# Softmax on negated scores in a windowed attention: the sink as the start of the minimum and as one more column

## The chip, the core and the metric

The kernel runs on one core of a Trainium2 chip. The time is device microseconds from start to end of the program. Five engines of the core work side by side, each through its own queue and in its order: PE (matrix products), DVE (VectorE), ACT (ScalarE), POOL (GpSimd) and SP, which here only issues DMAs. The profile tells for every instruction its start, its duration and, from the semaphores, what ended a wait before it.

## The reference, cut to what matters

One layer of a bidirectional encoder is computed for two requests, a prompt of 512 tokens and a sample of 1024, with shared weights: RMSNorm, one projection, windowed attention beside a convolution branch, an output projection, a feed-forward part with a short convolution, a last RMSNorm. The attention, which is what the change touches, is:

```python
sc = einsum("bnqhgd,bnkhd->bnhgqk", qb, kb) * (HEAD_DIM ** -0.5)
sc = sc + bias[None, None]
sc = where(mask, sc, NEG)                       # |q - k| <= 128 and inside the sequence
sk = sink.reshape(N_KV, GROUP, 1, 1)
m = maximum(max(sc, axis=-1, keepdims=True), sk)
p = exp(sc - m)
denom = sum(p, axis=-1, keepdims=True) + exp(sk - m)
p = (p / denom)
o = einsum("bnhgqk,bnkhd->bnqhgd", p, vb)
```

Queries come in blocks of 128. Each block sees its own 128 keys and the 128 on both sides (256 keys at the ends of a sequence, 384 elsewhere). There are 8 heads in 2 groups of 4, each group with its own keys and values. The sink is one number per head; it takes part in the maximum and in the denominator, and has no value row.

## The kernel before

All matrix products are made of operands split into a high and a low part: ACT writes the rounded high part (L143, L548), and POOL or DVE subtracts it from the original to get the low part (L144, L549). PE then multiplies high by high, high by low and low by high, which is why most PE lines come in threes (L250, L251 and L253 for the projections and the up-projection; L813 to L815 for the down-projection). For a chunk of weights, `split` has ACT cast 128x1024 elements (L143) and POOL subtract (L144); PE needs POOL's result for L253.

The work is written as Python generators which are advanced in turn. The main line is the projection (`step`) and later the prompt's feed-forward part (`ffn_step`); attention, the normalisation of the convolution branch and the output projection are put between its matrix products by `tick`, at rates given by constants. So the prompt's attention, 4 blocks, stands beside the sample's projection (about 115 to 255 us of the profile), and the sample's, 8 blocks, beside the prompt's feed-forward part (about 390 to 760 us). The depthwise convolution over 31 taps, which DVE does tap by tap (L293), runs in between as well, with some taps on ACT and POOL (L285, L286). After that come the output projection of the sample (L641 to L643) and the sample's feed-forward part, in a form with fewer products.

The order of instructions in each engine's queue up to there is not written out by hand. A planner takes the program and orders each engine's instructions by its own estimate of durations, in the limits of the dependences. For the last part (from L1202 on) the order on PE is by hand and the planner orders the other engines.

A unit of attention is one block of queries for one group of 4 heads; there are 12 blocks and 2 groups, 24 units. For a unit, `scores` does this for each of the 4 heads: two matmuls give the scores in a PSUM bank (L502); one DVE instruction adds the bias, writes the sum to a tile `p` in SBUF, and keeps the row's maximum (L505, followed in the trace by a short read of the accumulator). After all four heads:

- L512 (DVE) takes the minimum of the negated maximum and the negated sink, for four columns at once: `negm`, the negative of the softmax's maximum.
- L513 (DVE) adds the sink to it: the exponent of the sink's term.
- L515 (ACT, four times) takes the exponential of each head's row with `negm` as bias and sums it into `den`.
- L517 (ACT) takes the exponential of the sink's term, L518 (DVE) adds it to `den`, L519 (DVE) takes the reciprocal.
- L523 and L525 multiply each head's row by it: three heads on ACT and one on POOL in the prompt, and one on DVE, two on ACT, one on POOL in the sample.

`values` then transposes the rows on PE (L546), splits them (L548, L549), multiplies by the values (L560, L561) and combines the result (L568 to L572). A unit's scores are made before the values of the unit ahead of it, so that PE has other work while the softmax runs.

Other lines that the prediction speaks of: L775 is a tap of the short convolution in the feed-forward part, on DVE, which reads a PSUM bank; PE's next product into that bank (L250) waits for it. L127 is a small scaling on POOL, L319 a small memset on POOL, L323 the gate of the convolution branch on DVE. `qsd` is a buffer in DRAM through which the queries go.

The tiles in SBUF come from fixed slots, taken when a tile is made and given back when its last holder goes; a new tile's first writer waits until the former tile's readers are done.

## Time and profile before

| | |
|---|---|
| median of 3 runs | 1566.0 us (1565.88 to 1571.18) |
| profiled execution | 1563.92 us |
| its span, first to last instruction | 1562.1 us |
| mean granted PE clock | 0.998 |
| instructions | 20200 |
| attention of the prompt, 8 units | about 115 to 255 us |
| attention of the sample, 16 units | about 390 to 760 us |

A line of the page or of a view names the source line, the engine, the operation and the tiles (out<-in, buffer numbers left out), then shapes and the number of instructions. In a view of one line the three durations are minimum, median and maximum in nanoseconds. In a view of waits "PE a L561 <- DVE h L549: 1.7, 3, 1.2" says that PE's line 561, writing a tile of kind a, waited for DVE's line 549 for 1.7 us in total, in 3 waits, the longest 1.2 us. In a timeline the first number is the start in us from the span's start, the second the duration. Matmuls overlap in their pipeline: one of 128x512 shows a duration of about 0.39 us but the next starts some 0.23 us after it.

### The profile page before, as it was taken

What the parts mean: (1) busy time and instruction counts of PE and PEld (TensorE: products, weight loads), DVE (VectorE), ACT (ScalarE), POOL (GpSimd) and SP (SyncE); (2) the same over time, 40 slices, a digit from 0 to 9 for tenths busy, and PEclk for the clock granted to TensorE, in tenths of its full rate; (3) what the DMA queues carried; (4) which work ended last, traced back from release to release, by engine and by line L of the source; (5) the groups of instructions that cost most, each with busy time, mean ns of one, the idle gap of its engine ahead of it and who ended that gap; (6) DMA issues with size and microseconds to landing.
All of it is one profiled execution on the core that took longest, in us unless ns stands there. A gap on an engine that the chain in (4) does not pass through costs nothing. (4 is left out here: it accounts for less than half of the span.)

```text
span 1562.1 us, 20200 instructions
## 1 busy us (share of the span) xinstructions
PE 1519.2 (97%) x6909; PEld 1234.5 (79%) x6909; DVE 1200.5 (77%) x1731; ACT 799.2 (51%) x1426; POOL 729.5 (47%) x559
## 2 busy tenths in 40 slices
PE   8899899999998999999999999999999999999998
PEld 6787788887886778888877887888888878788886
DVE  7999868638989996756675768777777777877795
ACT  4634566335565655656554455444444445544364
POOL 7651344238576676656653324555555554000135
PEclk9999999999999999999999999999999999999999
DMA  7573246446331333333657222333333332694642
GB/s 229 157 201 95 87 118 165 130 133 166 108 117 64 108 108 109 99 97 95 212 164 230 82 68 78 111 102 101 101 102 102 101 102 101 206 354 144 219 142 108
DMA packets 209771, 207.62 MB, mean 133 GB/s; under 512 B 11156, under 2 KB 150748, under 8 KB 209541
## 3 DMA queue, kind: packets, MB, share of 16 engines
q1 hardware_dynamic: 209669, 206.35, 42.0%
q8 instruction: 54, 0.88, 0.2%
q14 instruction: 48, 0.39, 0.1%
HBM read 158.84 MB, written 48.51 MB: 133 GB/s over the span
## 5 line engine op out<-in xcount | busy, mean ns | idle before, releaser
L144 POOL TENSOR_TENSOR q<-q,q 128x1024 fp32r<-128x1024 f32 x72 | 175.0, 2436 | 68.8 <-ACT q L143 33.8
L921 POOL TENSOR_TENSOR q<-q,q 128x512 fp32r<-128x512 f32 x82 | 114.0, 1401 | 155.9 <-ACT q L1031 151.4
L250 PE MATMUL u<-h,q 128*128 128x512 f32 x400 | 158.5, 396 | 3.6 <-DVE h L775 2.8
L251 PE MATMUL u<-h,q 128*128 128x512 f32 x400 | 158.6, 396 | 0.6 <-DVE h L212 0.6
L253 PE MATMUL u<-h,q 128*128 128x512 f32 x384 | 151.9, 396 | 2.2 <-POOL q L144 2.2
L1045 PE MATMUL w<-h,q 128*128 128x512 f32 x372 | 147.4, 396 | 3.1 <-ACT h L1126 1.7
L1047 PE MATMUL w<-h,q 128*128 128x512 f32 x372 | 145.9, 392 | 0.6 <-POOL q L921 0.6
L293 DVE SCALAR_TENSOR_TENSOR c<-c,cvw,c 128x512 f32<-128x512 f32 x184 | 138.1, 750 | 2.4
L1046 PE MATMUL w<-h,q 128*128 128x512 f32 x350 | 137.6, 393 | 0.0
L143 ACT CAST q<-q 128x1024 fp32r<-128x1024 f32 x72 | 75.6, 1050 | 77.5 <-POOL q L144 44.6
L918 POOL TENSOR_TENSOR q<-q,q 128x1024 f32<-128x1024 f32 x8 | 23.8, 2989 | 182.9 <-DVE q L918 171.2
L250 PE MATMUL b<-h,q 128*128 128x512 f32 x256 | 102.1, 399 | 2.9 <-DVE d L323 2.9
L1354 PE MATMUL w<-h,h 128*128 128x512 f32 x264 | 103.8, 393 | 0.0
L1356 PE MATMUL w<-h,h 128*128 128x512 f32 x264 | 103.6, 392 | 0.0
L921 DVE TENSOR_TENSOR h<-h,h 128x512 fp32r<-128x512 f32 (+1 forms) x128 | 92.3, 764 | 11.4 <-ACT h L925 9.2
L251 PE MATMUL b<-h,q 128*128 128x512 f32 x256 | 100.7, 393 | 0.0
L253 PE MATMUL b<-h,q 128*128 128x512 f32 x256 | 100.5, 393 | 0.0
L1355 PE MATMUL w<-h,h 128*128 128x512 f32 x244 | 95.9, 393 | 0.0
L921 POOL TENSOR_TENSOR c<-q,c 128x512 fp32r<-128x512 f32 x46 | 71.0, 1557 | 51.8 <-ACT c L1031 51.8
L250 PEld LDWEIGHTS u<-h,q 128*128 128x128 f32 x400 | 75.6, 189 | 20.4 <-DVE h L775 3.3
L925 ACT CAST h<-h 128x512 fp32r<-128x512 f32 x101 | 58.7, 618 | 59.4 <-DVE h L921 27.0
L251 PEld LDWEIGHTS u<-h,q 128*128 128x128 f32 x400 | 75.5, 189 | 16.4 <-DVE h L212 1.6
(457 smaller groups left out, 4278.8 us busy)
## 6 DMA issues: line engine op xcount, KB each, us to landing
q<-in_w_up SPq DMA_DIRECT2D x88, 512.0 KB
h<-in_w_down SPq DMA_DIRECT2D x90, 256.0 KB
ga<-q SPq DMA_DIRECT2D x64, 256.0 KB
h<-ga SPq DMA_DIRECT2D x57, 256.0 KB
q<-in_w_in SPq DMA_DIRECT2D x28, 512.0 KB
q<-in_x_sample SPq DMA_DIRECT2D x15, 512.0 KB
h<-qsd SPq DMA_DIRECT2D x24, 256.0 KB
q<-ga SPq DMA_DIRECT2D x20, 256.0 KB
```

Of the source, the lines that this page charges most:

```text
L144: (nc.vector if dve else nc.gpsimd).tensor_tensor(lo[:], raw[:], hi[:].bitcast(F32), op=ALU.subtract)
L250: nc.tensor.matmul(out, whi[:, kc, :], hi[:], start=(kc == 0), stop=False)
L251: nc.tensor.matmul(out, whi[:, kc, :], lo[:], start=False, stop=False)
L253: nc.tensor.matmul(out, wlo[:, kc, :], hi[:], start=False, stop=(kc == KC - 1))
L293: nc.vector.scalar_tensor_tensor(acc[:], src(t), w(t), acc[:], op0=ALU.mult, op1=ALU.add)
L921: (eng or nc.vector).tensor_tensor(out, a, b, op=ALU.subtract)
L1045: nc.tensor.matmul(out, whi[:, s], hi[:], start=(start and c == 0), stop=False, **go)
L1046: nc.tensor.matmul(out, whi[:, s], lo[:], start=False, stop=False, **go)
L1047: nc.tensor.matmul(out, wlo[:, s], hi[:], start=False, stop=(stop and c == 3), **go)
L1354: nc.tensor.matmul(out, sh[:, c], th[:], start=(p == 0), stop=False)
L1355: nc.tensor.matmul(out, sh[:, c], tl[:], start=False, stop=False)
L1356: nc.tensor.matmul(out, sl[:, c], th[:], start=False, stop=(p == NPAIR - 1))
```

## The change

The scores' sum with the bias is written negated, and the row's minimum is kept instead of its maximum. That minimum starts from the negated sink of the head, given as a pointer to one number per partition, so it is `negm` at once. The row's tile is one column longer, and POOL copies the negated sink into that column. The exponential is taken with a scale of -1 over the longer row, so its sum, the denominator, has the sink's term in it. L512, L513, L517 and L518 have nothing left to do and are gone, and so are the two small tiles `mx` and `es`. The transposes and products after it use the row without its last column, as before.

```diff
-        mx, negm, den, es = sm(GRP), sm(GRP), sm(GRP), sm(GRP)
-        hs = slice(kv * GRP, (kv + 1) * GRP)
+        negm, den = sm(GRP), sm(GRP)
         pr = []
         for j in range(GRP):
             h = kv * GRP + j
...
-            p = sb.tile([3 * P])
+            p = sb.tile([3 * P + 1])
+            nc.gpsimd.tensor_copy(p[:, nk:nk + 1], nsink[:, h:h + 1])
             nc.vector.tensor_tensor_reduce(
-                out=p[:, :nk], in0=sc[:, :nk], in1=bias[h][:, off:off + nk], scale=1.0,
-                scalar=-3.0e38, op0=ALU.add, op1=ALU.max, accum_out=mx[:, j:j + 1])
+                out=p[:, :nk], in0=sc[:, :nk], in1=bias[h][:, off:off + nk], scale=-1.0,
+                scalar=nsink[:, h:h + 1], op0=ALU.add, op1=ALU.min, accum_out=negm[:, j:j + 1])
             pr.append(p)
...
-        nc.vector.scalar_tensor_tensor(negm[:], mx[:], -1.0, nsink[:, hs], op0=ALU.mult, op1=ALU.min)
-        nc.vector.tensor_tensor(es[:], sinkb[:, hs], negm[:], op=ALU.add)
+
         for j in range(GRP):
-            nc.scalar.activation(pr[j][:, :nk], pr[j][:, :nk], AF.Exp, bias=negm[:, j:j + 1],
+            nc.scalar.activation(pr[j][:, :nk + 1], pr[j][:, :nk + 1], AF.Exp, scale=-1.0, bias=negm[:, j:j + 1],
                                  accum_out=den[:, j:j + 1])
-        nc.scalar.activation(es[:], es[:], AF.Exp)
-        nc.vector.tensor_tensor(den[:], den[:], es[:], op=ALU.add)
         nc.vector.reciprocal(den[:], den[:])
```

## The prediction

> **What bounds the kernel now.** First the page's busy times, to see which engine has no room.

> ```profile
> PE 1519.2 (97%) x6909; PEld 1234.5 (79%) x6909; DVE 1200.5 (77%) x1731; ACT 799.2 (51%) x1426; POOL 729.5 (47%) x559
> ```

> PE is the bound: nothing in the change touches a matmul, so only time in which PE stands still can be won or lost. Second, the busy times by stretch, since the change acts only where attention runs: 8 units beside the projections (115 to 255 us) and 16 beside the prompt's feed-forward part (390 to 760 us). Columns: stretch, its length, busy us of PE, PEld, DVE, ACT, POOL, granted clock, DMA share, GB/s.

> ```profile
> 115.00:255.00 140.00, 133.53 (x648) 109.27 (x647) 111.89 (x235) 78.80 (x181) 46.78 (x35) 1.00 0.40 111
> 390.00:624.00 234.00, 225.79 (x1031) 183.23 (x1030) 208.38 (x374) 136.66 (x264) 153.72 (x99) 0.99 0.33 103
> 624.00:760.00 136.00, 136.00 (x648) 112.97 (x647) 88.28 (x168) 77.98 (x155) 80.35 (x50) 1.00 0.37 115
> 470.00:478.00 8.00, 5.12 (x15) 3.84 (x16) 8.00 (x12) 3.02 (x5) 2.57 (x2) 0.79 0.00 0
> ```

> PE loses 6.5 us in the first stretch, 8.2 in the second (where DVE is 89% busy), nothing in the third (DVE 65%). So at most about 15 us, and the time lost at a reduced clock, stand open to any change of attention. Third, who ended PE's waits, in 390 to 624 and then in 115 to 255 (us in total, times, longest).

> ```profile
> PE u L250 <- DVE h L775: 2.8, 1, 2.8
> PE a L561 <- DVE h L549: 1.7, 3, 1.2
> PE a L502 <- DVE h L570: 1.2, 2, 0.7
> PE a L502 <- DVE h L549: 1.0, 1, 1.0
> PE a L502 <- DVE s L505: 0.9, 1, 0.9
> ```

> ```profile
> PE a L560 <- ACT h L548: 1.9, 1, 1.9
> PE u L502 <- DMA h<-qsd: 1.7, 1, 1.7
> PE u L502 <- DMA qsd<-h: 1.4, 1, 1.4
> ```

> In the second stretch 7.6 of PE's 8.2 us are ended by DVE: DVE's lateness is what PE pays for. In the first stretch most is ended by ACT and DMAs.

> **The change, part by part.** *Three DVE operations per unit go* (L512 the negated minimum, L513 the sink's exponent, L518 its addition to the denominator), 24 of each. Their rows (min/median/max ns), and beside them the reciprocal L519 on the same four columns, with one tensor input instead of two:

> ```profile
> L512 DVE SCALAR_TENSOR_TENSOR s<-s,nsink x24: 138/163/2186, 122.2 to 747.9; 128x4 f32<-128x4 f32 x24
> L513 DVE TENSOR_TENSOR s<-sinkb,s x24: 145/161/2316, 123.0 to 750.6; 128x4 f32<-128x4 f32 x24
> L518 DVE TENSOR_TENSOR s<-s,s x24: 149/156/1069, 126.8 to 752.9; 128x4 f32<-128x4 f32 x24
> L519 DVE RECIPROCAL s<-s x24: 161/172/178, 127.9 to 753.1; 128x4 f32<-128x4 f32 x24
> ```

> The medians say that they are small; the maxima say that they are sometimes held for up to 2.2 us, and L519 never is. In the crowded stretch their sums (busy us, mean ns) are

> ```profile
> L513 DVE TENSOR_TENSOR s<-sinkb,s 128x4 f32<-128x4 f32 x10 | 7.6, 760 | 0.1
> L512 DVE SCALAR_TENSOR_TENSOR s<-s,nsink 128x4 f32<-128x4 f32 x10 | 7.3, 732 | 0.1
> L518 DVE TENSOR_TENSOR s<-s,s 128x4 f32<-128x4 f32 x10 | 4.5, 451 | 1.3 <-ACT s L517 1.3
> ```

> that is 19.4 us of DVE in ten units, of which 30 x 0.16 = 4.8 is work and 14.6 is being held. Two places show what the hold does to PE (start us, duration us):

> ```profile
> 515.56 2.05 DVE L513 TENSOR_TENSOR s<-sinkb,s 128x4 f32<-128x4 f32 x1
> 517.54 0.68 DVE L549 TENSOR_TENSOR h<-a,h 128x512 fp32r<-128x512 f32 x1
> 518.27 0.50 PE L561 MATMUL a<-h,h 128*128 128x512 f32 x1 [1.24 <-DVE h L549]
> ```

> ```profile
> 462.36 0.98 DVE L512 SCALAR_TENSOR_TENSOR s<-s,nsink 128x4 f32<-128x4 f32 x1
> 463.92 1.80 DVE L513 TENSOR_TENSOR s<-sinkb,s 128x4 f32<-128x4 f32 x1
> 470.64 2.15 DVE L525 TENSOR_SCALAR h<-h,s 128x384 f32<-128x384 f32 x1
> 472.71 0.74 DVE L775 SCALAR_TENSOR_TENSOR h<-u,fw,h 128x511 f32<-128x511 f32 x1
> ...
> 463.31 2.39 POOL L144 TENSOR_TENSOR q<-q,q 128x1024 fp32r<-128x1024 f32 x1
> 470.22 2.35 POOL L144 TENSOR_TENSOR q<-q,q 128x1024 fp32r<-128x1024 f32 x1
> ...
> 473.50 0.61 PE L250 MATMUL u<-h,q 128*128 128x512 f32 x1 [2.75 <-DVE h L775]
> 477.25 0.39 PE L250 MATMUL u<-h,q 128*128 128x512 f32 x1
> 477.47 0.39 PE L251 MATMUL u<-h,q 128*128 128x512 f32 x1
> ```

> At 515 the held L513 stands directly ahead of the subtraction for which PE waits 1.24 us: that wait goes. At 463.92 L513 ends (465.72) just when POOL's L144 ends (465.70): the hold lasts as long as POOL's instruction. L512 and L513 take 2.78 us there, 0.32 without a hold, so DVE is 2.5 us late in what follows. But L525, which stays, is held in the same way behind the L144 of 470.22 (2.15 us, where its row below has a median of 0.42), and L775 is behind L525. Of PE's 2.75 us there, the 1.7 that L525 causes may stay; between 1.05 and 2.75 goes, and I take 1.5, nearer the lower end because the L525 row is the direct one. After this pause PE runs slowly: nine matmuls from 473.50 to 477.25 take 3.75 us against 9 x 0.22 = 2.0, with a granted clock of 0.79 in those 8 us. These 1.7 us go if the pause becomes shorter. Of the other 4.8 us ended by DVE (1.7 + 1.2 + 1.0 + 0.9) I take two thirds, 3.2, since the relief is spread over ten units and the waits stand among them; ends: 1.2 (the one shown) and 4.8. Sum of this part: -6.4, from -2.3 to -9.3. In 115 to 255, where PE waits for ACT and DMAs, I take 0.

> ```profile
> L525 DVE TENSOR_SCALAR h<-h,s x16: 353/420/2147, 405.4 to 753.3; 128x384 f32<-128x384 f32 x12, 128x256 f32<-128x256 f32 x4
> L517 ACT ACTIVATE s<-s x24: 188/190/207, 124.9 to 752.1; 128x4 f32<-128x4 f32 x24
> L319 POOL MEMSET c<- x4: 110/110/111, 1.4 to 1.7; 128x15 f32 x4
> L127 POOL TENSOR_SCALAR s<-s x24: 190/191/1132, 6.0 to 871.2; 128x1 f32<-128x1 f32 x24
> L323 DVE SCALAR_TENSOR_TENSOR c<-h,b x4: 677/683/687, 130.0 to 352.5; 128x512 f32<-128x512 f32 x4
> L293 DVE SCALAR_TENSOR_TENSOR c<-c,cvw,c x184: 735/752/756, 183.9 to 592.1; 128x512 f32<-128x512 f32 x184
> PE u L253 <- POOL q L144: 2.2, 3, 1.2
> ```

> *The sink's exponential on ACT goes*: 24 x 0.19 = 4.6 us, on an engine 51% busy; nothing on PE's side. The Exp has one column more, which I take as nothing; its scale of -1 is a constant, as is the present 1.

> *The reduction L505 gets a pointer in place of a constant.* The nearest rows are two-operand steps with one operand in PSUM: 683 ns with a constant (L323), 752 with a pointer (L293). So +0.07 us each, 96 x 0.07 = 6.7 us of DVE over the kernel, some 2.8 in the crowded stretch; the lower end is 0. Against 19.4 removed there this leaves 16.6, and the sum above already stays short of all. That L293 is never held (maximum 756 in 184) says that a pointer beside one SBUF tensor doesn't make an instruction wait for POOL.

> [...]

> *POOL gets 96 copies of one column* (four per unit), no DMA is added or moved. Bounds: 0.11 us (L319, writes only) and 1.13 (the longest L127); I take 0.19, the median of L127, which also reads a column: 18 us over the kernel, 7.6 in the crowded stretch, where POOL has 80 of 234 us free. In POOL's queue each copy may wait for its slot, and the weights' low halves (L144) stand behind it; PE's multiplications by them (L253) wait behind those, 2.2 us in the whole kernel now. Each Exp now waits for its copy and its own reduction instead of the unit's L512; behind it on ACT stand the casts L548, for which PE waits 1.9 us in 115 to 255. These two rows are what such waits cost now; for new ones I take their mean, +2.0. Ends: 0 (an earlier Exp pays for them), and 8.6 (both rows again, 4.1, and one more pause like that of 470 with its slow stretch, 2.75 + 1.7).

> The program is ordered by a planner, so queues move: of the 6,910 PE instructions 2,589 stand elsewhere in the changed program, none before the 545th or after the 4,037th, and by 130 places at most. The later part, planned by hand on PE, is unaltered and I take 0 for it.

> Sum: -6.4 + 2.0 = -4.4. The profiled execution took 1563.9, so 1559.5; it lies 2.1 us below the median of the runs (1566.0), hence 1561.6.

> **The rivals.** *Larger relief.* The shorter chain (no wait between reduction and Exp) also takes away the ACT-ended wait of 1.9 and much of the rest in 115 to 255: -9.3 - 1.9 and more, to -15: 1551 to 1557. For it: DVE is 80% busy in 115 to 255 too. Against: two DMA waits there don't depend on DVE.

> *Hidden anyway.* L525 and other steps remain to be held by POOL, so DVE only waits at the next of these: -2 to +3, 1564 to 1569. The 2.15 us of L525 speak for it, the wait at 518.27 against it.

> *Slower: copies hold up POOL.* A copy whose slot PE hasn't freed stands at POOL's head with an L144 behind it, PE reaches L253 first and pauses; a pause like that of 470 costs 2.75 + 1.7 = 4.5 us. Beside a relief of 6.4, it takes four such pauses to be slower by over 0.5% (18 - 6.4 = 11.6, 1578) and two to be level; without the relief two do it. For it: PE's order is rearranged, with little slack known. Against: PE waited for L144 only 2.2 us, and POOL is a third idle.

> *The pointer counts as a second SBUF input.* Then L505 is held like L512: 0.73 - 0.16 = 0.57 us, forty times 23 us of DVE in the crowded stretch, more than the 19.4 removed. That and the pointers' 2.8 leave DVE 6.4 us worse; at the present ratio of PE's lost time to hold ((8.2 + 1.7) / 14.6 = 0.68) PE loses 4.4 more, and with the new waits' 2.0 it is 1572, a few us more with the other two stretches. L293 speaks against it. [...]

> **How the numbers follow.** A forecast of -2 to -9: 0.48; larger relief 0.17; hidden 0.13; held POOL 0.17; pointer 0.05. A measurement of this kernel tells about 0.5% (7.8 us) from no change, so the limits are 1558.2 and 1573.8. Faster: larger relief and a third of the forecast's band, 0.33. Slower: three quarters of held POOL and two thirds of the pointer case, 0.16. The rest, 0.51, is the same. The range leaves out a tenth on each side: 1550 (nearly all PE waits of both stretches gone) to 1574; the likeliest case alone (2 to 9 us less) spans 1557 to 1564.

> **What would show it.** Right: DVE's busy time in 390 to 624 falls from 208 to some 192 us, PE's DVE-ended waits there from 7.6 to 3 or less, a clock of 1.00 throughout, L505 at 0.55 + 0.07 us, 96 copies near 0.19 us. Wrong: new PE waits ended by POOL L144 or ACT L548, a new stretch with a clock below 1, L505 with durations of 1 to 2 us, or copies near 1 us.

## The result, and the profile after

The changed kernel takes 1576.53 us (median of 7 runs, 1571.88 to 1580.22), the kernel before 1565.09 beside it (1561.54 to 1571.18, 7 runs). The ratio is 1.0065, with a 95% interval from 1.0042 to 1.0087: slower by 11 us, where 4 us less was forecast. The profiled execution took 1574.2 us with a span of 1572.4. In the changed kernel some line numbers are others: L501 are the scores, L504 the copies, L505 the reduction, L514 the Exp, L516 the reciprocal, L520 and L522 the scaling on ACT and on DVE (before: L523 and L525); from there on they are three lower (L543 the transposes, L545 and L546 the split, L557 and L558 the value products, L772 the tap of the short convolution, L791 and L792 two additions and products of 128x512 on DVE).

The page's busy times of the changed kernel:

```profile
PE 1526.1 (97%) x6909; PEld 1239.3 (79%) x6909; DVE 1180.7 (75%) x1659; ACT 801.3 (51%) x1402; POOL 745.2 (47%) x655
```

DVE has 20 us less to do, PE 7 us more with the same 6909 products, some of which run at the lower clock seen below. The busy times by stretch, of the changed kernel (stretch, length, busy us of PE, PEld, DVE, ACT, POOL, granted clock, DMA share, GB/s):

```profile
115.00:255.00 140.00, 128.80 (x607) 103.95 (x605) 106.97 (x207) 73.95 (x165) 46.50 (x57) 0.97 0.34 97
390.00:624.00 234.00, 227.50 (x1042) 186.72 (x1041) 201.19 (x348) 140.02 (x254) 168.31 (x145) 0.99 0.33 104
246.00:262.00 16.00, 11.94 (x45) 8.56 (x44) 14.27 (x27) 9.81 (x22) 1.63 (x4) 0.79 0.52 127
```

In 390 to 624 PE is a little better off than before (227.50 against 225.79). The loss is in 115 to 255: PE does 607 products there in place of 648, and most of it lies in the 16 us from 246 on, where PE starts 45 products at a clock of 0.79. To see where time goes without regard to stretches, take the start of the k-th matmul in the trace and subtract that of before (this delay is what k stands for below): 0 at k = 1000 (224 us), +3.4 at 1080, +10.1 at 1120 (259 us), +14.7 at 2000 (460 us), +7.3 at 2600 (592 us), +10.9 at 4000 and after. So about 10 us are lost between 224 and 259 us, 4 to 5 more up to 460, 7 are won back between 460 and 592, and another 3 go at 595.

Who ended PE's waits in the changed kernel (those largest in total), first in 115 to 258, then in 345 to 640:

```profile
PE u L501 <- DMA h<-qsd: 2.8, 2, 2.4
PE a L543 <- ACT h L617: 1.4, 1, 1.4
PE a L557 <- ACT q L545: 1.3, 1, 1.3
PE a L557 <- ACT h L545: 1.1, 2, 0.9
PE a L558 <- DVE q L546: 0.9, 2, 0.7
PE b L253 <- POOL q L144: 0.9, 1, 0.9
```

```profile
PE a L501 <- DMA q<-ksd: 2.5, 1, 2.5
PE b L810 <- ACT h L143: 2.2, 2, 1.5
PE a L543 <- DVE h L546: 2.2, 1, 2.2
```

The 2.8 us pause behind the tap of the short convolution is gone, as forecast. But there are new waits for the splits (L545, L546), for the normalisation of the convolution branch (L617) and for a DMA. The place at 247 us in PE's timeline (start, duration, wait in brackets):

```profile
246.62 0.39 PE L253 MATMUL b<-h,q 128*128 128x512 f32 x1
246.85 0.60 PE L614 MATMUL a<-ident,h 128*128 128x128 f32 x4
247.20 0.48 PE L501 MATMUL u<-h,h 128*128 128x256 f32 x2
249.10 0.33 PE L543 MATMUL a<-ident,h 128*128 128x128 f32 x1 [1.42 <-ACT h L617]
...
251.07 0.80 PE L557 MATMUL a<-q,h 128*128 128x512 f32 x1 [1.31 <-ACT q L545]
252.57 0.79 PE L558 MATMUL a<-q,h 128*128 128x512 f32 x1 [0.71 <-DVE q L546]
...
254.84 0.79 PE L250 MATMUL b<-h,q 128*128 128x512 f32 x1 [0.62 <-DVE q L328]
```

PE's queue holds here, without one projection product between them, the transposes of the convolution branch (L614), scores (L501), a unit's transposes (L543) and that unit's value products (L557, L558). By the waits in brackets the transposes L543 start only when ACT (L617) has worked on what L614 wrote, and the value products when ACT and DVE have split the transposes (L545, L546). So PE stands, and then its products take 0.6 to 0.8 us in place of 0.39. In the kernel before the same transposes start at 242.75 and the value products at 245.28, with nine projection products between and no wait; PE is busy all 16 us from 246 to 262, with 80 products. The reader sees a change of order, not of work. Whether it is the cause is what the experiments ask.

### The profile page after: what moved, and what is told of

Same layout as the page of the kernel before. It is cut to its first block, busy times and chain, and to the rows that moved or that the text cites. A ratio compares the mean times of both kernels' runs of the same rounds, so it can differ in the third digit from the quotient of the medians.

```text
span 1572.4 us, 20204 instructions
## 1 busy us (share of the span) xinstructions
PE 1526.1 (97%) x6909; PEld 1239.3 (79%) x6909; DVE 1180.7 (75%) x1659; ACT 801.3 (51%) x1402; POOL 745.2 (47%) x655
## 5 line engine op out<-in xcount | busy, mean ns | idle before, releaser
L144 POOL TENSOR_TENSOR q<-q,q 128x1024 fp32r<-128x1024 f32 x72 | 174.7, 2430 | 85.1 <-ACT q L143 51.7
L251 PE MATMUL u<-h,q 128*128 128x512 f32 x400 | 159.0, 398 | 0.4 <-DVE h L212 0.4
L250 PE MATMUL u<-h,q 128*128 128x512 f32 x400 | 158.2, 396 | 1.0 <-DVE h L212 0.9
L253 PE MATMUL u<-h,q 128*128 128x512 f32 x384 | 152.2, 397 | 1.1 <-POOL q L144 1.1
L293 DVE SCALAR_TENSOR_TENSOR c<-c,cvw,c 128x512 f32<-128x512 f32 x184 | 138.0, 750 | 2.7
L250 PE MATMUL b<-h,q 128*128 128x512 f32 x256 | 102.8, 402 | 4.4 <-DVE d L323 2.9
L253 PE MATMUL b<-h,q 128*128 128x512 f32 x256 | 102.0, 399 | 0.9 <-POOL q L144 0.9
L251 PE MATMUL b<-h,q 128*128 128x512 f32 x256 | 102.0, 399 | 0.0
L250 PEld LDWEIGHTS u<-h,q 128*128 128x128 f32 x400 | 75.8, 189 | 17.8 <-DVE h L212 1.1
L251 PEld LDWEIGHTS u<-h,q 128*128 128x128 f32 x400 | 75.7, 189 | 17.1 <-DVE h L212 2.2
```

What stands on the lines that cost most here:

```text
L144: (nc.vector if dve else nc.gpsimd).tensor_tensor(lo[:], raw[:], hi[:].bitcast(F32), op=ALU.subtract)
L250: nc.tensor.matmul(out, whi[:, kc, :], hi[:], start=(kc == 0), stop=False)
L251: nc.tensor.matmul(out, whi[:, kc, :], lo[:], start=False, stop=False)
L253: nc.tensor.matmul(out, wlo[:, kc, :], hi[:], start=False, stop=(kc == KC - 1))
L293: nc.vector.scalar_tensor_tensor(acc[:], src(t), w(t), acc[:], op0=ALU.mult, op1=ALU.add)
```

## The experiments

Theory A: the work itself becomes less, and what costs is the order in which the planner now issues PE's products. Theory B: the changed work (copies, pointer, other waits) costs, and the order only follows it.

### The same work in the old order, and the old work in the new order

An order can be imposed without a semaphore, by telling the planner that each instruction of an engine comes after the one ahead of it in the wanted list. The edit is the same in all runs that do so:

```diff
+        _same_order(tc)
...
+        for a, b in zip(order[:-1], order[1:]):
+            tc.add_manual_dep(byname[f"I-{b}"], f"I-{a}",
+                              mybir.DependencyInfo(mybir.DependencyClass.NoSync, mybir.DependencyReason.DATA),
+                              reason="order")
```

> The changed kernel, with PE's queue put into the order that it has in the kernel before (issue order only, no added wait); the other engines are ordered by the planner as always. Theory A (the 10 us are lost because the planner's new order on PE puts the last units' transposes and value products back to back, with no projection matmuls between): the loss at 224 to 275 us goes and the relief of DVE stays, so 3 to 8 us less than before. Theory B (the work itself: Exps waiting for POOL's copies, copies at the head of POOL's queue, the longer reduction): the loss stays, 8 to 12 us more than before.

Measured: 1556.25 us (1555.21 to 1559.54), ratio to before 0.9945, from 0.9928 to 0.9963. This beats both kernels.

> The kernel before, with PE's queue put into the order that it has in the changed kernel; its operations are those of before, all of them. Theory A: slower than before by 8 to 14 us, lost at the same place in PE's order (between the 1,000th and the 1,200th matmul). Theory B: within 3 us of before, since none of the new work is there.

Measured: 1587.12 us, ratio 1.0135 (1.0111 to 1.0159): 22 us more than the kernel before, beyond the 8 to 14 expected. The delay stands at +10.5 at k = 1200, the place that Theory A named, and grows on behind it: +17.6 at 1800, +25.8 at 2800.

> The changed kernel, with the instructions that it shares with the kernel before put in that kernel's order on all five engines; POOL's copies stand where the planner puts them. Theory A: as with PE alone or better, 3 to 9 us less than before; what is left is the price of the operations themselves (fewer held DVE instructions, 0.06 us more for each reduction, copies on POOL). Theory B: 8 to 12 us more than before.

Measured: 1556.68 us, ratio 0.9942 (0.9918 to 0.9965). The order of the other four queues adds nothing to that of PE.

The changed kernel in PE's old order, two stretches and the waits of PE in 390 to 624:

```profile
115.00:255.00 140.00, 134.91 (x647) 110.03 (x646) 108.71 (x211) 79.04 (x173) 50.42 (x59) 0.99 0.40 111
390.00:624.00 234.00, 230.84 (x1072) 189.88 (x1071) 202.53 (x354) 143.38 (x264) 166.92 (x144) 1.00 0.34 105
```

```profile
PE a L501 <- DVE h L567: 1.7, 2, 1.1
PE b L810 <- DVE q L813: 0.8, 1, 0.8
PE a L501 <- DVE s L505: 0.5, 1, 0.5
```

647 products again in the first stretch, 1072 in place of 1031 in the second, and DVE-ended waits of 3.0 us where there were 8.0 (the prediction's 7.6 leaves out 0.4 at L813). Its matmuls stand at +0.2 until k = 2080 (about 462 us) and at -5.6 by 2160, -9.0 by 2600, -8.5 to the end. Theory A holds, in both directions: the work of the change is worth some 9 us (1565.2 less 1556.25), and its order costs 20 (1576.5 less 1556.25).

### Where in the order the loss lies

Two runs exchange the order at matmul 1250, where both orders have issued the same set. (Written here as slices; each kernel holds its finished list.)

```diff
-        order = as_after[:1250] + as_after[1250:]
+        order = as_before[:1250] + as_after[1250:]    # front_as_before
+        order = as_after[:1250] + as_before[1250:]    # rest_as_before
```

> The changed kernel, with the first 1250 matmuls of PE's queue in the order of the kernel before (up to about 260 us) and all others in the planner's new order; both orders hold the same 1250 matmuls there, so the seam adds nothing. Theory A1 (the new order's loss is local and adds up: about 9.8 us of the 19 or so stand ahead of matmul 1250, the rest behind it): 1566 to 1568 us, milestones level with before up to matmul 1250. Rival A2 (a delay ahead is given back or doubled later, since it decides how the later queues meet): not between 1564 and 1570; if the whole loss hangs on the front, 1557 to 1560, if on what follows, 1573 to 1577.

> The mirror image: the first 1250 matmuls in the planner's new order, all later ones in the order of before. A1: +9.8 against the kernel with the whole queue as before (1556.2), so about 1566, and a delay of some 10 us at matmul 1200 which stays to the end. A2: the delay at matmul 1200 is there but half of it or more is given back later (1557 to 1561), or it grows (over 1571).

Measured: front as before 1563.11 us, ratio 0.9988 (0.9977 to 0.9999); rest as before 1566.37, ratio 1.0010 (0.9997 to 1.0023). Against 1556.25 with the whole old order, a new front costs 10.1 us, as A1 expected, and a new rest 6.9, where A1 expected 10 to 12 (1566 to 1568). Together they cost 20.3, 3.3 more than the sum. The intervals of the four ratios are too wide to say that this remainder is there, and in the profiled executions the parts add up (12.4 and 7.4 against 19.0 at k = 6800). With the new front and old rest, the delay is +12.1 at k = 1200 and +11.9 at 2100, so it isn't given back.

### The one place at 247 us

> The changed kernel's own order on PE with one edit: of the 18 projection matmuls directly ahead of the four conv_norm transposes L614, nine are put behind L614 and L501, ahead of the four transposes L543, and nine between these and the four value products L557/L558. Nothing else moves on any queue by hand. Theory W2 (PE waits there for its own just finished transposes to come back through ACT and DVE, and then runs at a reduced clock): from matmul 1092 to 1116 some 6 us go, the waits of 1.4 and 1.3 us on L545/L617 with them, no stretch below full clock there: about 1570. If the waits come from ACT and DVE being late by themselves: the waits stay in another place, 1574 to 1577.

```diff
-        18 x projection  L614 x4  L501 x2                  L543 x4                  L557 L558 L557 L558
+                         L614 x4  L501 x2  9 x projection  L543 x4  9 x projection  L557 L558 L557 L558
```

(This shows PE's queue at the place, not code; a projection is one product of L250, L251 or L253.) Measured: 1568.66 us, ratio 1.0020 (1.0008 to 1.0032), that is 7.9 us less than the changed kernel, for 18 products moved by up to ten places. PE's timeline there:

```profile
242.64 0.66 PE L614 MATMUL a<-ident,h 128*128 128x128 f32 x4 [0.44 <-DVE h L608]
243.05 0.49 PE L501 MATMUL u<-h,h 128*128 128x256 f32 x2
243.38 0.40 PE L250 MATMUL b<-h,q 128*128 128x512 f32 x1
...
245.45 0.27 PE L543 MATMUL a<-ident,h 128*128 128x128 f32 x1
...
247.74 0.40 PE L253 MATMUL b<-h,q 128*128 128x512 f32 x1
247.97 0.40 PE L557 MATMUL a<-q,h 128*128 128x512 f32 x1
...
250.52 0.50 PE L250 MATMUL b<-h,q 128*128 128x512 f32 x1 [1.30 <-DVE q L328]
```

The waits of 1.42, 1.31 and 0.71 are gone and the products of 128x512 take 0.4 to 0.5 us; one wait, for L328, has grown from 0.62 to 1.30, and one of 0.44 is new. From k = 1092 to 1116 the delay grows by 1.7 us, where it grew by 6.6. ACT and DVE were not late by themselves; PE had nothing to do while they answered.

> The changed kernel in its own new order on PE, except matmuls 1001 to 1104 (224 to 253 us), which stand as in the kernel before; both orders hold the same 104 there, 101 of them in other places. Theory W (the front's 10 us arise in this window): milestones level with before from 1000 to 1120 within 1 us, and 1566 to 1568. If the loss follows from what stands after it (matmuls 1105 to 1250): still +6 or more at matmul 1200, 1573 to 1577.

```diff
+        order = as_after[:1000] + as_before[1000:1104] + as_after[1104:]
```

Measured: 1569.29 us, ratio 1.0036 (1.0025 to 1.0047): 7.2 us less than the changed kernel, where 8.5 to 10.5 were expected. The slow place at 247 us is gone (clock 1.00 from 246 to 262), but a new wait of 2.9 us appeared at 229 us (L602, for a DMA of the convolution branch), where a stretch of one order was put into the other. The delay is at +5.7 from k = 1020, not level as Theory W said, and at +7.3 at 1200, which taken alone is the rival's sign (+6 or more). But 4.5 us of it arise at the new wait, between k = 1000 and 1010; from 1020 to 1250 this kernel loses 1.6 us and the changed kernel 9.5. So the window holds most of the front's loss, which this run shows less cleanly than the run before.

### What the three DVE operations were worth

Two kernels put three operations per unit back on DVE, with results that nobody reads, in the changed kernel with PE's old order: in one the forms of L512, L513 and L518, with two tensors of SBUF each, in the other three reciprocals, with one.

```diff
+        nc.vector.scalar_tensor_tensor(x0[:], negm[:], -1.0, nsink[:, hs], op0=ALU.mult, op1=ALU.min)
+        nc.vector.tensor_tensor(x1[:], sinkb[:, hs], negm[:], op=ALU.add)
...
+        nc.vector.tensor_tensor(x2[:], den[:], x1[:], op=ALU.add)
```

or

```diff
+        nc.vector.reciprocal(x0[:], negm[:])
+        nc.vector.reciprocal(x1[:], negm[:])
...
+        nc.vector.reciprocal(x2[:], den[:])
```

> The changed kernel with PE's queue as before, and per unit three operations on DVE whose results nobody reads: the forms of L512, L513 and L518 (two tensors of SBUF each, four columns). Nothing waits for them but what stands behind them on DVE. Theory H (the gain of 8.5 us is the time for which such operations were held behind POOL): the hold comes back (some 10 us or more of DVE in 390 to 624 us, single ones of 1 to 2 us) and the time with it: 1562 to 1567. Rival C (the gain is the shorter chain from reduction to Exp, without L512 and the sink's exponential between): stays at 1556 to 1559 though the operations are held.

> As the run with three operations of two inputs, but all three are reciprocals on four columns (one tensor input, 0.17 us each, as many instructions). Theory H: never held (maxima under 0.2 us), 5 us more of DVE in 390 to 624, and a time of 1556 to 1559. If the number of operations on DVE is what costs, and not the hold: the same time as with the two-input forms, 1562 or more. Rival C: 1556 to 1559 for both.

Measured: 1565.84 us with two inputs (ratio 1.0007, 0.9998 to 1.0017) and 1562.16 with one (0.9985, 0.9976 to 0.9994). The first is what Theory H expected, the second is not: 6 us more than without the operations, though its reciprocals at 470 us took 0.15 to 0.18 us, where one of the operations with two inputs took 2.06 at 471.94. The trace shows why the pair could not settle it: DVE's queue was left to the planner, and in both kernels it now put seven taps L293 in a row ahead of a unit's last reductions, after which PE waits 4.8 us (like before's pause at 473 us, but longer). So all five queues were put in the order of before, with the extra operations in the places of L512, L513 and L518:

> The changed kernel with all five queues in the order of the kernel before, and in the places of L512, L513 and L518 three operations of the same forms whose results nobody reads. Against the kernel before there are left: the pointer in the reduction, 96 copies on POOL, no exponential of the sink on ACT, and no wait of Exp for L512. In the run with such operations that left DVE's order to the planner, DVE's queue had moved too (seven taps L293 ahead of a unit's last reductions, then a pause of 4.8 us), with one-input forms as with two, so that the two runs did not tell hold from order. Theory H (the hold behind POOL makes most of the 8.5 us): held again by some 10 us or more in 390 to 624, the pause at about 470 us is back, 1562 to 1566. Theory Q (the gain is that DVE has less to issue ahead of the late steps, held or not): the same as its sister with reciprocals. Rival C (the shorter chain is the gain): 1556 to 1559, no pause.

> The same with three reciprocals in the same places. Theory H: no hold on them, at most +1.5 for 5 us of work of DVE in the stretch, 1556 to 1559, no pause at 470. Theory Q: the same time as with two-input forms, 1562 to 1566. Rival C: 1556 to 1559 for both.

Measured: 1566.60 us with two inputs (ratio 1.0006, 0.9997 to 1.0015), 1552.68 with one (0.9924, 0.9897 to 0.9952), which is below the 1556 to 1559 of Theory H. The same number of operations in the same places, 14 us apart. With two inputs (stretch; PE's waits in it; the three groups in it as busy us, mean ns):

```profile
390.00:624.00 234.00, 224.93 (x1024) 182.60 (x1024) 210.80 (x373) 135.77 (x254) 158.42 (x138) 0.99 0.33 103
```

```profile
PE u L250 <- DVE h L777: 2.8, 1, 2.8
PE a L563 <- DVE h L551: 1.7, 3, 1.2
PE a L503 <- DVE s L507: 1.6, 2, 1.4
```

```profile
L520 DVE TENSOR_TENSOR s<-s,s 128x4 f32<-128x4 f32 x10 | 7.7, 768 | 0.2 <-ACT h L518 0.2
L515 DVE SCALAR_TENSOR_TENSOR s<-s,nsink 128x4 f32<-128x4 f32 x10 | 7.0, 696 | 0.1
L516 DVE TENSOR_TENSOR s<-sinkb,s 128x4 f32<-128x4 f32 x10 | 5.9, 591 | 0.0
```

and with one:

```profile
390.00:624.00 234.00, 232.68 (x1080) 191.60 (x1079) 203.77 (x384) 142.66 (x265) 167.67 (x146) 1.00 0.35 108
```

```profile
PE a L503 <- DVE h L572: 0.6, 1, 0.6
PE a L503 <- DVE s L507: 0.5, 1, 0.5
```

```profile
L520 DVE RECIPROCAL s<-s 128x4 f32<-128x4 f32 x10 | 1.7, 170 | 0.3 <-ACT h L518 0.3
L515 DVE RECIPROCAL s<-s 128x4 f32<-128x4 f32 x10 | 1.7, 168 | 0.1
L516 DVE RECIPROCAL s<-s 128x4 f32<-128x4 f32 x10 | 1.6, 162 | 0.0
```

20.6 us of DVE against 5.0 for thirty small operations; the difference of 15.6 is hold. The pause of 2.8 us behind the tap (here L777) is there with the one, absent with the other, as are the waits for the low half (L551). Theory Q (the count of operations) and Rival C (the shorter chain from reduction to Exp) fall: both kernels have the count, both have the short chain. What the kernel lost to L512, L513 and L518 was the time for which POOL kept them standing. In the kernel before 53 of their 72 instructions take 0.14 to 0.17 us, the other 19 take 0.51 to 2.32, and each of the 19 ends 14 to 23 ns after an instruction of POOL has ended. DVE's and POOL's timeline of the kernel with two inputs shows two such ends:

```profile
463.62 1.77 DVE L516 TENSOR_TENSOR s<-sinkb,s 128x4 f32<-128x4 f32 x1
...
470.31 2.14 DVE L527 TENSOR_SCALAR h<-h,s 128x384 f32<-128x384 f32 x1
```

```profile
462.98 2.39 POOL L144 TENSOR_TENSOR q<-q,q 128x1024 fp32r<-128x1024 f32 x1
...
469.89 2.35 POOL L144 TENSOR_TENSOR q<-q,q 128x1024 fp32r<-128x1024 f32 x1
```

L516 ends at 465.39 and POOL's L144 at 465.37; L527 ends at 472.45, the next L144 at 472.24. L527, the scaling on DVE, reads only one tensor and a pointer from SBUF and takes 2.14 us all the same, where the median of this line in the kernel before (L525) is 0.42: the count of input tensors alone doesn't tell which operations are held here.

Not all of the 14 us is the hold of the three. The changed kernel without any such operations, with all five queues in the old order, is at 1556.68 us; it still pauses 2.2 us behind that tap (here L772) and has a clock of 0.79 from 470 to 478, where the kernel with the reciprocals has no such pause and a clock of 1.00. So about 10 us (1566.60 less 1556.68) are the hold of the three operations; the other 4 are not clear of noise (0.9897 to 0.9952 and 0.9918 to 0.9965 overlap). Where the scaling falls beside POOL's work is luck: with two inputs it starts at 470.31 and takes 2.14 us, in the changed kernel with PE's queue alone as before it starts at 464.05 and takes 0.41.

### The copies alone

> The changed kernel without POOL's copies: the sink's term is left out of the denominator, the Exp reads the row without the further column; ordered anew by the planner, which again puts the last transposes and value products of the prompt back to back. Theory A: still 5 to 12 us more than before, lost at the same place. Theory B, if the copies are the cause: 4 to 7 us less than before.

```diff
-            nc.gpsimd.tensor_copy(p[:, nk:nk + 1], nsink[:, h:h + 1])
```

Measured: 1568.55 us, ratio 1.0022 (1.0010 to 1.0034). That is 3.3 us more than before, where Theory A expected 5 to 12 and Theory B 4 to 7 less. The loss named by Theory A is there (the delay grows by 5.5 us between k = 1092 and 1116), without any copy. But the run doesn't price the copies: without them the planner makes a third order, with waits of its own for the splits. So the copies were added to the kernel before, once with the planner free and once with all queues as they were:

```diff
-            p = sb.tile([3 * P])
+            p = sb.tile([3 * P + 1])
+            nc.gpsimd.tensor_copy(p[:, nk:nk + 1], nsink[:, h:h + 1])
```

> The kernel before with one part of the change alone: tiles one column longer and the 96 copies on POOL into that column, which nobody reads. The planner is free; 1734 matmuls stand elsewhere, and four transposes of a unit come directly ahead of its four value products at the place where the changed kernel loses 10 us. Theory A (the order is what costs): 1571 to 1579, with the loss between matmuls 1000 and 1200. Theory B (the copies cost by holding up POOL, and the order is harmless): the same as the run with all queues as before, whatever that is.

> The same kernel with all that it shares with the kernel before in the order of before, on all five queues; the copies stand where the planner puts them between. Theory A: the copies by themselves cost 0 to 2 us (0.19 us each, 7.6 us of POOL in 390 to 624): 1565 to 1568. Theory B: 1570 or more.

Measured: 1571.33 us free (ratio 1.0045, 1.0031 to 1.0059), 1566.27 in the old order (1.0011, 0.9999 to 1.0022). The copies themselves measure as 1.7 us, with an interval that just takes in nothing; the order that they lead the planner to costs 5 more, less than the changed kernel's own order and at the low end of what A expected. It is lost in two places, +3.5 by k = 1300 (2.6 of it by 1200, where A looked for all of it) and another 3.5 between 2300 and 3100.

## Why the prediction was wrong

*The step that failed* is "The program is ordered by a planner, so queues move". It was stated, with 2,589 of the 6,910 PE instructions in other places, and then got no price of its own: new waits of every kind were one term, +2.0 with ends 0 and 8.6, sized by two rows of waits in the old order. The order alone is worth some 20 us (1576.53 against 1556.25). The rows of the old order could not bound it, for they show what is left where projection products cover the turns through ACT and DVE, and the new order took the cover away: a unit's transposes and value products now follow one another directly. The prediction gave only how many instructions moved and how far; what decided was what lies between a transpose and the product that needs it, which the two orders show without a run.

*"In 115 to 255 I take 0"* failed for the same reason: the stretch had no wait for DVE to win, but most to lose, and 10 of the 20 us are lost from 224 to 259 us.

*Three DVE operations go, -6.4 (from -2.3 to -9.3).* The mechanism was right and the size near the upper end: -9.0 in the old order with all the rest of the change, and 10 us between the kernels with and without three held operations. The pause at 473.5 was put at -1.5 of 2.75, since the scaling on DVE stays; with PE's queue alone as before the pause went altogether, with all queues as before 2.2 us of it stayed, and in the kernel with two inputs the scaling of 2.14 us stands directly ahead of that tap, so the reason was sound and the figure a matter of the queue. The slow stretch behind it went with the pause in the first of these (a clock of 1.00 from 466 to 482); in the second the clock stayed at 0.79 from 470 to 478. In the changed kernel as it stands the same relief is seen, from +14.7 at k = 2000 to +7.3 at 2600; it only comes after the loss.

*DVE from 208 to 192 us* failed in part: 201 to 203. In the changed kernel eight more taps L293 fall into the stretch (100 in place of 92, 5.9 us more), and part of the hold moved to other operations with two tensors in SBUF, which the sum had not listed. L791 (before: L794) in 390 to 624, in the kernel before and then in the changed one:

```profile
L794 DVE SCALAR_TENSOR_TENSOR h<-h,h 128x512 f32<-128x512 f32 x11 | 7.8, 707 | 0.0
```

```profile
L791 DVE SCALAR_TENSOR_TENSOR h<-h,h 128x512 f32<-128x512 f32 x12 | 15.3, 1274 | 2.7 <-ACT h L790 2.7
```

At 0.68 us without a hold (the shortest L791 takes 678 ns) that is 0.3 us of hold before and 7.1 after. No wait of PE in this stretch is put down to L791. With PE's order the old one, where L791 is held for 3.7 us, the DVE-ended waits fell to 3.0 us, as forecast.

*The pointer, +0.07 us each,* was right, and so was the small chance (0.05) of the rival in which it counts as a second SBUF input. *The copies, 0.19 us each,* too. The changed kernel, minimum, median and maximum in ns:

```profile
L505 DVE CUSTOM_DVE_ANT_0 h<-a,h,nsink x80: 470/610/619, 120.0 to 756.6; 128x384 f32<-128x384 f32 x57, 128x256 f32<-128x256 f32 x23
L504 POOL COPY h<-nsink x92: 173/185/655, 108.6 to 756.1; 128x1 f32<-128x1 f32 x92
```

549 has become 610, and no reduction is held (the longest takes 0.62 us). The traces show a hold for two tensors in SBUF (L516 above, 1.77 us) and none for this reduction, which reads PSUM, one tensor and a pointer. The prediction's wording, that a pointer beside one SBUF tensor doesn't make an instruction wait, is too wide: the scaling L527 above, from SBUF to SBUF, has just these inputs and took 2.14 us. What sets the two forms apart, no run here shows.

*The rivals.* "Copies hold up POOL" named the right sign with the wrong mechanism: PE's one wait for L144 in 115 to 258 is 0.9 us, and the copies in the old order measure as 1.7 us. "Hidden anyway" was right only in that the hold found new operations. "Larger relief" (1551 to 1557) has the time of the change with the order kept, 1556.25, but by luck: its mechanism, a shorter chain that takes PE's waits out of 115 to 255, isn't seen, since the delay stays at +0.2 until k = 2080.

## What to carry to other kernels

Where a planner orders the queues, an edit has two prices, its work and the order that it leads to; here they were -9 and +20 us, and only runs with the order held fixed told them apart. Before any run, compare the two orders for chains that return to PE through another engine (transpose, split, product) and count the independent products between the links; where that count falls to zero, price each link at its full turn and add the slow clock after it (the next section says when). On DVE, remove first what has two tensors in SBUF beside long POOL instructions: a four-column operation of 0.16 us (L516 with two inputs, median 155 ns) took up to 2.44, and a reciprocal in its place at most 0.17 in 24. A single tensor is no safeguard in itself, as the scaling of 2.14 us shows.

## What the runs showed of the hardware

```profile
247.49:250.90 3.41, 0.84 (x6) 0.42 (x4) 3.34 (x8) 3.36 (x10) 0.18 (x1) 1.00 0.58 157
592.23:595.64 3.41, 1.27 (x6) 0.71 (x4) 3.41 (x7) 3.15 (x7) 3.00 (x2) 1.00 0.50 149
```

```profile
470.33:473.74 3.41, 0.66 (x3) 0.33 (x3) 3.41 (x4) 1.32 (x4) 2.24 (x1) 1.00 0.00 0
```

```profile
246.86:250.27 3.41, 2.36 (x10) 1.37 (x8) 3.41 (x8) 2.50 (x7) 0.18 (x1) 1.00 0.01 2
```

PE is busy 0.84, 1.27 and 0.66 of the 3.41 us in the first three, and a stretch at half rate follows each; in the fourth it is busy 2.36 us, and none follows. The traces of the kernel before and of the changed kernel, cut along their grids, have 906 such stretches at full clock. After each of the 8 in which PE was busy for less than 38%, the clock was 0.5 in the next; after none of the other 898, in which it was busy for 51% or more. So in these two traces what goes with the lower clock is how much of such a stretch PE is busy, and not how long one pause is, and the same pause costs more or less by where it falls: PE's wait of 2.92 us for L323 ends at 52.15 in the kernel before, across a step of its grid at 50.48, and no slow stretch follows; in the changed kernel it ends at 52.36, within the step from 49.51 to 52.92, and the clock is 0.5 in the next.
